# Swapping which down-projection units use paired result banks, spreading the last four activations over four units, and sharing the last stores between two queues

## The chip, the cores and the metric

The kernel runs on one core of a Trainium2 chip. A core has a matrix engine (PE, with its weight loads listed as PEld), a vector engine (DVE), an activation engine (ACT), a GpSimd engine (POOL) and a SyncE queue (SP) that here only issues DMA transfers. Each engine works through its own instructions in order and waits on semaphores for the others. Matrix products land in eight result banks on chip, which PE writes and DVE or ACT read; everything else lies in the big on-chip memory or in device memory.

The metric is the device time of one execution in microseconds. It is 2808.09 us for this kernel, the median of three runs (2815.43, 2808.08 and 2808.09).

## The reference, cut to what matters

One layer of a streaming encoder for 512 prompt frames and 64 sample frames: modulated norms, a token mixer with two kinds of recurrence, and a feed-forward part. Only the feed-forward part and the final norm matter here:

```python
def conv_ffn(h, st, w_up, ffn_conv_w, ffn_conv_b, w_down):
    gate, val = jnp.split(h @ w_up, 2, axis=-1)
    gate_c, new_st = causal_dwconv(gate, st, ffn_conv_w)
    act = jax.nn.silu(gate_c + ffn_conv_b) * val
    return act @ w_down, new_st
...
    x = x + g2 * f
...
    y = rmsnorm(x, final_norm)
```

`w_up` is 2048 x 11264, `w_down` is 5632 x 2048, all in float32. The results are `y_prompt` (512 x 2048), `y_sample` (64 x 2048) and the new states.

## The kernel before, in words

**Float32 by parts.** Each operand of a product is split into a rounded part and a rest. The rounded part is made by ACT (`wh`, line 1630), the rest by a subtraction on DVE (`wl`, line 1632), and a product of two split operands is three matmuls: lines 1725, 1726 and 1727 for the projections of the feed-forward part, lines 647 and 649 elsewhere.

**Units.** The up- and the down-projection use a two-by-two Strassen-Winograd scheme with seven products (`c` = 0 to 6) per unit. Units `t` = 0 to 43 are the up-projection (`NFF` = 44). Units 44 to 75 are the down-projection: four groups `g` = 0 to 3 of eight units `u` = 0 to 7, where a group takes ten of the 44 slices of 128 activations and a unit takes one pair of 128-wide output columns. A product of the down-projection is 5 x 3 matmuls. The products of unit `t` are issued in the order 0, then product 6 of unit `t` - 1, then 2, 1, 3, 4, 5 (`DOWN_ORDER`); unit 44 has no such guest, so its products 0 and 2 stand next to each other.

**Result banks.** A unit has three results x, y, z. Products 0 and 3 go to x, products 2, 4 and 6 to y, products 1 and 5 to z. All up units, and the even down units, take three single banks from `bank()`, which has four of them (tile name `bank`). The odd down units take two tiles from `pgt()`, each a pair of banks (tile name `g`): x and y are the two halves of the first pair, z is half of the second. `pgt()` has two such pairs and serves the stage after the down-projection too. After each product `down_out` adds the result to an output tile: ACT copies (line 1919) where the target is new, which is so in group 0 alone, and DVE adds (line 1921) elsewhere. A later product may write a tile only after that. The framework that orders the instructions follows the priority of the written order, lets a ready instruction go first where one ahead of it isn't ready by its own estimate, and puts in the semaphore waits.

**Weights.** Two steps ahead of each product `up_prep` and `down_prep` make its `wh` and `wl`; DVE also forms the sums that the scheme needs (lines 1643, 1685, 1697 and 1700). The raw weights are loaded by SP (line 1622) into a ring of eight tiles (`raw_late`, list `raws`).

**Places.** The split activations that the products read lie in tiles called `slot`; a list `vacant` keeps the free places. In group 3 no further group is to be loaded, so `vacant` grows: it has nine entries when unit 69 begins and ten at unit 71.

**Group 3.** When a unit of group 3 is complete, `down_end` closes it in steps during the next unit: SP loads the residual (line 1942), POOL adds the last sums (lines 1943 and 1945), ACT scales (line 1953) and POOL adds the residual (line 1954). POOL has nothing to do in groups 0 to 2.

**Last activations.** The groups cover 40 slices. The last four go through a plain product in `final`. `acts` prepares them in the last unit, u = 7 of group 3, at product 2: for each it takes two vacant places and a tile of the ring, SP loads the slice (line 1963), ACT rounds it (line 1964) and DVE subtracts (line 1965).

**Final.** `final_begin` turns the two new convolution states on PE (line 2044). Then two halves `h` of the frames are done; in each, sixteen column blocks get four plain products into pair tiles from `pgt()` (line 2000), DVE scales and adds them (line 2005), and PE turns four blocks at a time (line 2056) for the final norm (lines 2058 to 2061). At the end of a half each of three blocks of frames (128, 128 and 32 rows) gets its factor, four tiles of it are scaled in turn by DVE (line 2072) and ACT (line 2070), and SP stores each right behind its scaling (lines 2075 and 2077): twelve stores for each half.

Of the kernel before, what the change touches and what calls it, by code (L numbers as in the profile page):

```python
# [21 lines left out]
HP, HS, HT = 256, 32, 288  # L22
NFF = 44
# [32 lines left out]
NPAIR = KD // 2  # L56
# [47 lines left out]
class Kern:  # L104
# [1603 lines left out]
    def up_product(self, t, c):  # L1708

        w = HZ if t < NFF else HT  # L1710
        if c == 0:
            if t < NFF or t % 2 == 0:
                banks = [self.bank()[:, :w] for _ in range(3)]
            else:
                a, b = self.pgt(), self.pgt()
                banks = [a[:, 0, :w], a[:, 1, :w], b[:, 0, :w]]
            self.a[t, "banks"] = banks
            self.a.pop((t - 2, "banks"), None)
        T, (wh, wl) = self.nc.tensor, self.a.pop((t, "w", c))
        ps = self.a[t, "banks"][(0, 2, 1, 0, 1, 2, 1)[c]]  # L1720
        n = NPAIR if t < NFF else NJ
        for j in range(n):
            hi, lo, _ = self.combos[c, j] if t < NFF else self.dn[(t - NFF) // NPAIR, c, j]

            T.matmul(ps, wh[:, j], hi, start=(c < 3 and j == 0), stop=False, skip_group_check=True)  # L1725
            T.matmul(ps, wh[:, j], lo, start=False, stop=False, skip_group_check=True)  # L1726
            T.matmul(ps, wl[:, j], hi, start=False, stop=(j == n - 1), skip_group_check=True)  # L1727
# [62 lines left out]
    def up(self):  # L1790
# [110 lines left out]
    def down_out(self, t, c):  # L1901

        nc = self.nc
        V, A, G = nc.vector, nc.scalar, nc.gpsimd
        g, u = divmod(t - NFF, NPAIR)
        x, y, z = self.a[t, "banks"]
        if g == 0 and c == 0:
            for m in (u, u + NPAIR):
                self.x1[m] = self.slot(self.vacant.pop(0), F32, HT)
            if u % 2 == 0:  # L1910
                self.sums_at = self.vacant.pop(0)
                s = self.slot(self.sums_at, F32, HT)
                self.sums[u], self.sums[u + 1] = s[:, 0], s[:, 1]
                self.sums_place.append(self.sums_at)
        lo, hi, p = self.x1[u], self.x1[u + NPAIR], self.sums[u]
        ps, dst, new = ((x, p, True), (z, hi[:, 1], True), (y, lo[:, 1], True), (x, lo[:, 0], True),
                        (y, hi[:, 1], False), (z, lo[:, 1], False), (y, hi[:, 0], True))[c]
        if g == 0 and new:
            A.activation(dst, ps, AF.Copy)
        else:  # L1920
            V.tensor_tensor(dst, ps, dst, op=ALU.add)  # L1921
        if u == NPAIR - 1:
            if c == 0 and g + 1 < NCH:
                self.want(g + 1)
            self.vacant += [self.dn.pop((g, c, j))[2] for j in range(NJ)]
            self.fill()
        if g == NCH - 1:
            if c == 2 and u == NPAIR - 1:
                self.last_acts = self.acts([self.vacant.pop(0) for _ in range(8)])
            if c == 6:  # L1930
                self.closing = self.down_end(u, lo, hi, p)
            if c in (6, 2, 1, 4):
                next(self.closing, None)
# [20 lines left out]
            G.tensor_tensor(x, x, xt[n], op=ALU.add)  # L1954
        yield

    def acts(self, places):

        nc, out = self.nc, []
        for n in range(4):  # L1960
            raw = self.raw_late()[:, :2 * HT].rearrange("p (h t) -> p h t", h=2)
            hh, hl = [self.slot(places[2 * n + i], F32R, HT) for i in range(2)]
            nc.sync.dma_start(raw, self.actd[NFF - 4 + n])
            nc.scalar.activation(hh, raw, AF.Copy)
            nc.vector.tensor_tensor(hl, raw, hh.bitcast(F32), op=ALU.subtract)
            out.append((hh, hl))
        return out

    def down(self):
        for _ in self.closing:  # L1970
# [8 lines left out]


    def final(self, acts, free):


# [65 lines left out]
    def final_part(self, h, q, blocks):  # L2049

        nc, o = self.nc, self.o
# [12 lines left out]
        for c0, n, y, ms in blocks:  # L2064
            V.tensor_reduce(ms[:n, 4:5], ms[:n, 0:4], axis=mybir.AxisListType.X, op=ALU.add)
            self.rsqrt(ms[:, 5:6], ms[:, 4:5], 1, n)
            for q in range(4):
                t = y[q][:n]
                if q % 2:
                    A.activation(t, t, AF.Copy, scale=ms[:n, 5:6])  # L2070
                else:
                    V.tensor_scalar_mul(t, t, ms[:n, 5:6])
                f = slice(q * 512, (q + 1) * 512)
                if c0 < HP:
                    nc.sync.dma_start(o["y_prompt"][0, h * HP + c0:h * HP + c0 + n, f], t)
                else:
                    nc.sync.dma_start(o["y_sample"][0, h * HS:(h + 1) * HS, f], t)


def layer_kernel(tc, i, o):  # L2080
# [216 lines left out]
```

## Time and profile before

| | |
|---|---|
| median of three runs | 2808.09 us |
| the profiled execution's own time | 2809.85 us |
| its span, first to last instruction | 2808.1 us |
| PE / DVE / ACT / POOL busy | 98% / 81% / 47% / 16% of the span |
| stretch 2272 to 2609 us (groups 0 to 2) | PE 336.12 of 337 us, DVE 262.80 |
| stretch 2609 to 2731 us (group 3) | PE 116.65 of 122 us, DVE 110.00 |
| stretch 2731 to 2797 us (final products) | PE 63.88 of 66 us |
| stretch 2797 to 2808 us (last stores) | PE idle |

The rows of a profile give a line of the kernel, its engine and operation, and `out<-in` by the names of the tiles. A pair tile is called `g`, a single bank `bank`. What stands in square brackets behind a row, or behind a bar in a group, is how long the engine was idle just before it, and what ended that. A matmul shows about 0.30 us, but they are pipelined and follow each other by about 0.13 us.

### The profile page before, as it was taken

To read this page: it belongs to the slowest core of one execution; us is meant where nothing else is said; L and a number is where in the kernel's file an instruction comes from. 1 tells how busy PE (TensorE), PEld (TensorE's weight loads), DVE (VectorE), ACT (ScalarE), POOL (GpSimd) and SP (SyncE) were. 2 spreads that over 40 slices of the span, in tenths; PEclk is the share of its full clock that TensorE was granted. 3 is DMA by queue.
4 is the path that set the end of the run, shared out by engine and by line. 5 is a ranking of instruction groups with operands and counts; after the bars stand their busy time and mean duration, and the time that the engine had idled before them with its cause. 6 is when DMAs were issued, how large, how long until landed. Compare 5 with 4: busy or idle time off the path is not lost.

```text
span 2808.1 us, 52899 instructions
## 1 busy us (share of the span) xinstructions
PE 2748.1 (98%) x20612; PEld 2668.6 (95%) x20612; DVE 2285.0 (81%) x3721; ACT 1314.0 (47%) x2314; POOL 458.7 (16%) x437
## 2 busy tenths in 40 slices
PE   7999999999999999999999999999999999999998
PEld 4799999999999999999999999999999999999997
DVE  4578787787877887678999999999998976888886
ACT  4255555464544442355454544444444444333453
POOL 0001000010000000000333333333333300000240
PEclk9999999999999999999999999999999999999999
DMA  9965455554644657633555555464646594673761
GB/s 304 336 195 158 137 140 144 144 154 133 181 142 122 176 166 211 196 101 114 154 162 158 171 157 177 143 184 142 191 142 183 154 299 150 186 235 101 222 173 69
DMA packets 650719, 478.15 MB, mean 170 GB/s; under 512 B 69962, under 2 KB 577093, under 8 KB 650469
## 3 DMA queue, kind: packets, MB, share of 16 engines
q1 hardware_dynamic: 637364, 461.31, 54.9%
q10 hardware_dynamic: 13104, 13.47, 1.6%
q8 instruction: 162, 2.65, 0.4%
q14 instruction: 89, 0.72, 0.1%
HBM read 397.73 MB, written 76.96 MB: 169 GB/s over the span
## 4 chain that ended last, share of the span: by engine, by line
PE 81%; DVE 8%; DMA 4%; issue 3%; ACT 2%; POOL 1%; SPq 0%; ACTq 0%; DVEq 0%; POOLq 0%
PE g L647 17%; PE bank L1726 14%; PE bank L1725 14%; PE bank L1727 14%; PE g L649 8%; PE bank L2219 4%; PE g L1725 2%; PE g L1727 2%; PE g L1726 2%; DVE acc L2203 2%; PE bank L2215 1%; PE bank L869 1%; DVE wl L1632 1%; DVE wl L2203 1%; DVE m L2179 1%
## 5 line engine op out<-in xcount | busy, mean ns | idle before, releaser
L1726 PE MATMUL bank<-slot,wh 128*128 128x290 f32 (+1 forms) x3024 | 903.3, 299 | 0.0
L1725 PE MATMUL bank<-slot,wh 128*128 128x290 f32 (+1 forms) x3024 | 900.8, 298 | 1.3 <-ACT sqa L1599 1.0
L1727 PE MATMUL bank<-slot,wl 128*128 128x290 f32 (+1 forms) x3024 | 894.7, 296 | 0.5 <-DVE wl L1632 0.4
L1727 PEld LDWEIGHTS bank<-slot,wl 128*128 128x128 f32 x3024 | 576.4, 191 | 1.6 <-DVE wl L1632 1.6
L1726 PEld LDWEIGHTS bank<-slot,wh 128*128 128x128 f32 x3024 | 573.7, 190 | 0.1
L1725 PEld LDWEIGHTS bank<-slot,wh 128*128 128x128 f32 x3024 | 568.7, 188 | 4.4 <-ACT sqa L1599 1.3
L647 PE MATMUL g<-hh,wh 128*128 128x288 f32 x2048 | 473.1, 311 | 1.0 <-ACT ts L2203 0.8
L1630 ACT ACTIVATE wh<-raw 128x1024 fp32r<-128x1024 f32 (+1 forms) x304 | 280.4, 923 | 363.1 <-PE bank L1726 263.0
L649 PE MATMUL g<-hh,wl 128*128 128x288 f32 x2048 | 441.9, 297 | 1.7 <-DVE wl L1027 1.7
L647 PE MATMUL g<-hl,wh 128*128 128x288 f32 x2048 | 442.4, 297 | 0.0
L1632 DVE TENSOR_TENSOR wl<-raw,wh 128x1024 fp32r<-128x1024 f32 (+1 forms) x304 | 371.4, 1222 | 73.0 <-ACT wh L1630 69.4
L1630 ACT ACTIVATE wh<-s 128x1024 fp32r<-128x1024 f32 (+1 forms) x228 | 210.7, 926 | 290.4 <-DVE s L1643 103.3
L647 PEld LDWEIGHTS g<-hh,wh 128*128 128x128 f32 x2048 | 325.2, 190 | 21.8 <-issue 15.1
L649 PEld LDWEIGHTS g<-hh,wl 128*128 128x128 f32 x2048 | 330.6, 189 | 5.1 <-issue 3.1
L647 PEld LDWEIGHTS g<-hl,wh 128*128 128x128 f32 x2048 | 330.6, 189 | 3.2 <-issue 2.3
L1632 DVE TENSOR_TENSOR wl<-s,wh 128x1024 fp32r<-128x1024 f32 (+1 forms) x228 | 250.4, 1100 | 14.5 <-ACT wh L1630 13.5
L2203 ACT ACTIVATE wh<-raw 128x1024 fp32r<-128x1024 f32 x135 | 142.6, 1057 | 197.6 <-PE g L647 193.9
L2203 DVE SCALAR_TENSOR_TENSOR acc<-aw,ct,acc 128x512 f32<-128x512 f32 x284 | 201.2, 744 | 3.1 <-DMA aw<-in_w_ada_dram 3.0
L2203 DVE TENSOR_TENSOR wl<-raw,wh 128x1024 fp32r<-128x1024 f32 x135 | 164.8, 1222 | 47.1 <-ACT wh L2203 44.3
L1849 POOL TENSOR_TENSOR j<-j,j 128x288 f32<-128x288 f32 (+1 forms) x120 | 184.4, 1543 | 85.6 <-ACT j L1853 83.1
L1725 PE MATMUL g<-slot,wh 128*128 128x288 f32 x560 | 167.1, 299 | 3.8 <-DVE slot L1921 3.8
L1726 PE MATMUL g<-slot,wh 128*128 128x288 f32 x560 | 165.4, 296 | 0.0
(341 smaller groups left out, 4061.8 us busy)
## 6 DMA issues: line engine op xcount, KB each, us to landing
raw<-in_w_up_dram SPq DMA_DIRECT2D x176, 512.0 KB
raw<-in_w_in_dram SPq DMA_DIRECT2D x100, 512.0 KB
raw<-in_w_down_dram SPq DMA_DIRECT2D x128, 320.0 KB
aw<-in_w_ada_dram SPq DMA_DIRECT2D x79, 512.0 KB
slot<-cd SPq DMA_DIRECT2D x140, 288.0 KB
cd<-j SPq DMA_DIRECT2D x120, 288.0 KB
xr<-in_w_ada_dram SPq DMA_DIRECT2D x49, 512.0 KB
hraw<-in_w_ada_dram SPq DMA_DIRECT2D x40, 512.0 KB
```

The source lines that it names most:

```text
L647: T.matmul(ps[:, h if bank is None else bank, :n], wh, x[:, h, :n], start=f, stop=False)
L649: T.matmul(ps[:, h if bank is None else bank, :n], wl, ah[:, h, :n], start=False, stop=stop)
L869: T.matmul(ps[32 * k:32 * k + 32, :w], cs[:, k0 + k], got[n][k // per][:, k % per], start=(k0 == 0), stop=(k0 == KD - 4))
L1630: self.nc.scalar.activation(hi, src, AF.Copy)
L1632: self.nc.vector.tensor_tensor(lo, src, hi.bitcast(F32), op=ALU.subtract)
L1725: T.matmul(ps, wh[:, j], hi, start=(c < 3 and j == 0), stop=False, skip_group_check=True)
L1726: T.matmul(ps, wh[:, j], lo, start=False, stop=False, skip_group_check=True)
L1727: T.matmul(ps, wl[:, j], hi, start=False, stop=(j == n - 1), skip_group_check=True)
L1849: minus = lambda out, a, b: G.tensor_tensor(out, a, b, op=ALU.subtract)
L2179: return f(*a, **kw)
L2203: return f(*a, **kw)
L2219: return self.engine.matmul(out, *a, **kw)
```

## The change

- `up_product`: of the down units, the even ones now take the pair tiles and the odd ones the single banks. The number of units of either kind stays at sixteen. The first down unit (44) has pairs, the last (75) single banks.
- `act` takes the place of `acts`. It prepares one of the last four slices in each of the units u = 3, 4, 5 and 6 of group 3 (units 71 to 74), again at product 2. The raw slice goes to one of two vacant places used in turn, not to a tile of the weights' ring; the two places are given back after the fourth. ACT's rounding is now put behind the latest rounding of weights on ACT's queue. The instructions are the same four loads, four roundings and four subtractions.
- `final_part`: the scalings of all three blocks are written first and then the twelve stores. In the second half, five stores (the four of the 32-row block and the last of the second block) are issued by ACT, seven by SP. In the first half all twelve stay on SP.

```diff
-            if t < NFF or t % 2 == 0:
+            if t < NFF or t % 2:
                 banks = [self.bank()[:, :w] for _ in range(3)]
             else:
                 a, b = self.pgt(), self.pgt()
...
-        self.closing = iter(())
+        self.closing, self.last_acts = iter(()), []
...
-            if c == 2 and u == NPAIR - 1:
-                self.last_acts = self.acts([self.vacant.pop(0) for _ in range(8)])
+            if c == 2 and u >= 3 and u < NPAIR - 1:
+                self.last_acts.append(self.act(u - 3))
...
+    def act(self, n):
+
+        nc = self.nc
+        if n == 0:
+            self.act_places = [self.vacant.pop(0) for _ in range(2)]
+        raw = self.slot(self.act_places[n % 2], F32, HT)
+        hh, hl = [self.slot(self.vacant.pop(0), F32R, HT) for i in range(2)]
+        nc.sync.dma_start(raw, self.actd[NFF - 4 + n])
+        with self.tc.issue_after(self.round_of):
             nc.scalar.activation(hh, raw, AF.Copy)
+        nc.vector.tensor_tensor(hl, raw, hh.bitcast(F32), op=ALU.subtract)
+        if n == 3:
+            self.vacant += self.act_places
+        return hh, hl
...
+        for k, (c0, n, y, ms) in enumerate(blocks):
+            for q in range(4):
+                t = y[q][:n]
+                queue = nc.scalar if h == 1 and (k == 2 or (k, q) == (1, 3)) else nc.sync
                 f = slice(q * 512, (q + 1) * 512)
                 if c0 < HP:
-                    nc.sync.dma_start(o["y_prompt"][0, h * HP + c0:h * HP + c0 + n, f], t)
+                    queue.dma_start(o["y_prompt"][0, h * HP + c0:h * HP + c0 + n, f], t)
                 else:
-                    nc.sync.dma_start(o["y_sample"][0, h * HS:(h + 1) * HS, f], t)
+                    queue.dma_start(o["y_sample"][0, h * HS:(h + 1) * HS, f], t)
```

More of the change, by code (lines that the diff above doesn't have):

```diff
@@ L1955, in down_end @@
         yield
[L1957 to L1963, printed above, removed]
+    def act(self, n):
[6 more added lines that the diff above has]
+        with self.tc.issue_after(self.round_of):
             nc.scalar.activation(hh, raw, AF.Copy)
-            nc.vector.tensor_tensor(hl, raw, hh.bitcast(F32), op=ALU.subtract)
-            out.append((hh, hl))
-        return out
+        nc.vector.tensor_tensor(hl, raw, hh.bitcast(F32), op=ALU.subtract)
+        if n == 3:
+            self.vacant += self.act_places
+        return hh, hl
     def down(self):
```

## The prediction

> **What bounds the kernel now.** I read the page, then stretches by unit, then what PE waits for from 2600 us on, then the single rows around those waits. Nothing ahead of unit 44 (2272 us) is touched.
>
> ```profile
> PE 2748.1 (98%) x20612; PEld 2668.6 (95%) x20612; DVE 2285.0 (81%) x3721; ACT 1314.0 (47%) x2314; POOL 458.7 (16%) x437
> ```
>
> PE is the bound, so only time in which PE stands can be won. The next view has the stretches of units 69 to 74 one by one, and then unit 75 (columns: us; busy PE, PEld, DVE, ACT, POOL; granted clock; DMA share and GB/s).
>
> ```profile
> 2623.00:2638.00 15.00, 14.43 (x106) 13.86 (x105) 14.69 (x18) 6.67 (x11) 6.35 (x4) 1.00 0.58 158
> 2638.00:2652.00 14.00, 14.00 (x108) 14.00 (x107) 13.97 (x20) 6.89 (x11) 6.95 (x4) 1.00 0.53 136
> 2652.00:2667.00 15.00, 14.45 (x108) 14.12 (x107) 12.90 (x19) 6.88 (x11) 6.38 (x4) 1.00 0.50 128
> 2667.00:2681.00 14.00, 14.00 (x107) 14.00 (x107) 14.00 (x20) 6.89 (x11) 6.95 (x4) 1.00 0.53 138
> 2681.00:2696.00 15.00, 14.45 (x108) 14.12 (x107) 12.91 (x19) 6.88 (x11) 6.37 (x4) 1.00 0.50 128
> 2696.00:2710.40 14.40, 14.02 (x106) 13.79 (x105) 13.87 (x19) 8.05 (x14) 6.51 (x4) 1.00 0.48 129
> 2710.40:2731.40 21.00, 17.30 (x123) 16.23 (x123) 17.61 (x25) 13.26 (x21) 6.15 (x4) 1.00 0.80 233
> ```
>
> Units 70 and 72 (single banks) take 14 us with DVE busy throughout; 71 and 73 (pairs) take 15, PE stands for 0.55, and DVE comes out with about 2 us to spare. What PE waits for from 2600 us to the end (a last row of 0.2 us is left out), and the rows of five of these waits:
>
> ```profile
> PE g L1725 <- DVE slot L1921: 3.8, 5, 1.6
> PE g L647 <- DVE slot L1921: 1.5, 1, 1.5
> PE bank L1727 <- DVE wl L1632: 0.4, 1, 0.4
> ...
> 2631.80 0.37 PE L1725 MATMUL g<-slot,wh 128*128 128x288 f32 x1 [0.56 <-DVE slot L1921]
> 2656.78 0.37 PE L1725 MATMUL g<-slot,wh 128*128 128x288 f32 x1 [0.55 <-DVE slot L1921]
> 2716.32 0.37 PE L1725 MATMUL g<-slot,wh 128*128 128x288 f32 x1 [1.56 <-DVE slot L1921]
> 2721.16 0.37 PE L1725 MATMUL g<-slot,wh 128*128 128x288 f32 x1 [0.61 <-DVE slot L1921]
> 2731.41 0.51 PE L647 MATMUL g<-slot,wh 128*128 128x288 f32 x2 [1.54 <-DVE slot L1921]
> ```
>
> Only pair tiles (`g`) wait for the adding (L1921), never single banks: x and y share a tile, so product 2 waits until product 0 has been added, with one product (2 us) in between as cover. In single banks a result is next written two or three products later. The fifth wait of the 3.8 is unit 73's, 0.55 by the equal stretch. The pool is 3.8 + 1.5 + 0.4 = 5.7 us.
>
> Why the adding is late, in DVE's and POOL's rows at unit 71, and the last activations:
>
> ```profile
> 2654.95 1.32 DVE L1700 TENSOR_TENSOR s<-raw,s 128x640 f32<-128x640 f32 x1
> 2656.19 0.45 DVE L1921 TENSOR_TENSOR slot<-g,slot 128x288 f32<-128x288 f32 x1
> ...
> 2654.26 1.32 POOL L1943 TENSOR_TENSOR slot<-slot,slot 128x288 f32<-128x288 f32 x1 [2.61 <-DVE slot L1921]
> ...
> 2707.52 0.74 DVE L1965 TENSOR_TENSOR slot<-raw,slot 128x576 fp32r<-128x576 f32 x1
> 2718.66 1.98 DVE L1965 TENSOR_TENSOR slot<-raw,slot 128x576 fp32r<-128x576 f32 x1
> ...
> 2718.09 1.94 POOL L1945 TENSOR_TENSOR slot<-slot,slot 128x576 f32<-128x576 f32 x1 [2.96 <-DVE slot L1921]
> ...
> L1965 DVE TENSOR_TENSOR slot<-raw,slot 128x576 fp32r<-128x576 f32 x4 | 4.9, 1213 | 0.5 <-ACT slot L1964 0.5
> L1964 ACT ACTIVATE slot<-raw 128x576 fp32r<-128x576 f32 x4 | 2.7, 686 | 5.4 <-DMA raw<-actd 5.4
> ```
>
> The same subtraction takes 0.74 us alone and 1.98 us where a POOL instruction runs, ending 0.6 us after POOL does. Four of them take 4.9 us, all around unit 75, where the longest wait is.
>
> **The change part by part.**
>
> *Parity in group 3.* Units 69, 71, 73 and 75 lose their pairs and 68, 70, 72 and 74 get them. Unit 68 comes before POOL starts closing units, so nothing is late there: 0. For 70, 72 and 74 the row nearest is unit 71's 0.55 each, since DVE's work per unit doesn't depend on where results lie: 1.65 us come back. Bounds: 0, since a single-bank unit might leave DVE less behind, and 1.56, the worst of unit 75.
>
> *Activations.* One subtraction goes into each of the units 71 to 74. In 72 and 74 (now pairs) it comes at product 2, behind the wait, where DVE has its 2 us to spare: 0; without that spare room 0.74 each. In 71 and 73 (now single banks) DVE has nothing to spare, so it makes the next pair unit's wait 0.74 longer each: 1.5 us. The bounds for each of the four are 0 and 1.98. The roundings (0.69 on ACT, busy 7 of 14 us) and loads lie beside other work; without ACT's room they would add 0.69 each. What DVE loses around unit 75 is 4.9 us, and with single banks there the cover of the adding is two products; so the 1.56, the 0.61 and the 0.4 go. What is late next is the weights' rest (L1632), which stands in the same queue; I take 0 for it in unit 75 and 0.4 (its wait now) as its upper bound.
>
> *Start of `final`.* Its first products take a pair, which unit 74 has left long before; the 1.5 goes. What is late next is the first weights. Their tiles of the ring aren't taken by activations any more, so they load earlier: 0.
>
> Group 3 together: 1.65 + 1.5 - 5.7 = -2.55, and I add -0.35 for two pauses fewer, as PE also loses some 0.16 us in refilling at each (the matmul behind a pause shows 0.37 and not 0.30, and its successor is late too; this is my estimate): **-2.9 us**. Bounds: -5.7, and 1.65 + 4 x 1.98 - 5.7 = +3.9.
>
> *Start of the down-projection.* Unit 44 gets pairs, has no guest product, and its adding is a copy on ACT that stands behind other ACT work:
>
> ```profile
> 2274.46 0.30 PE L1725 MATMUL bank<-slot,wh 128*128 128x288 f32 x1
> 2276.46 0.29 PE L1725 MATMUL bank<-slot,wh 128*128 128x288 f32 x1
> 2277.01 0.40 PE L1727 MATMUL bank<-slot,wl 128*128 128x288 f32 x1
> ...
> 2276.15 0.38 ACT L1919 ACTIVATE slot<-bank 128x288 f32<-128x288 f32 x1
> 2276.14 0.82 DVE L1632 TENSOR_TENSOR wl<-s,wh 128x640 fp32r<-128x640 f32 x1
> ```
>
> Product 2 began at 2274.46 and product 1 at 2276.46. With pairs product 2 can't begin before product 0's copy ends at 2276.53: 2.07 us later. Product 1, in the other pair, could go first, but its rest of weights is ready only at 2276.96, so that way doesn't help much. What goes in return is product 1's own wait for that rest (2277.01 instead of 2276.73, 0.28). Upper bound 2.1; lower 0, if the new order has the copy ahead on ACT. I take **+1.3**, nearer to the upper end, which is the row. The other pair units of groups 0 to 2 have one product of cover as now; no row shows a wait there, and their number is the same: 0.
>
> *Stores.* The last twelve on SP, what feeds them, and the DMA engines in steps of 1 us:
>
> ```profile
> 2798.95 4.48 SPq L2075 DMA_DIRECT2D out_dram<-y  x8
> 2803.53 2.18 SPq L2077 DMA_DIRECT2D out_dram<-y  x4
> ...
> 2798.44 3.78 ACT L2070 ACTIVATE y<-y,fms 128x512 f32<-128x512 f32 x6 [1.71 <-POOL fms L2233]
> ...
> 2800.00:2801.00 1.00, 0.00 (x0) 0.00 (x0) 0.89 (x3) 1.00 (x3) 0.00 (x0) 0.50 1.01 379
> 2804.00:2805.00 1.00, 0.00 (x0) 0.00 (x0) 0.00 (x0) 0.00 (x0) 0.00 (x0) 0.50 1.01 385
> 2805.00:2806.00 1.00, 0.00 (x0) 0.00 (x0) 0.00 (x0) 0.00 (x0) 0.00 (x0) 0.50 0.96 281
> 2806.00:2807.00 1.00, 0.00 (x0) 0.00 (x0) 0.00 (x0) 0.00 (x0) 0.00 (x0) 0.50 0.44 100
> ```
>
> Issuing ends at 2805.71. With seven on SP (2798.95 + 7 x 0.56 = 2802.9) and five on ACT behind its scalings (2802.2 + 5 x 0.55 = 2805.0, or less), issuing ends 0.7 us earlier or more. But the transfers fill the DMA engines from 2800 to 2806; only the 0.04 and 0.56 us unused in the last two steps can go. So **-0.5 us**, between 0 and -0.6.
>
> The Trainium skill ("DMA: Bandwidth & Descriptors", section "Issuing engines are not separate DMA queues") says that transfers from any issuing engine run on the same sixteen DMA engines and that several issuers save only issue time. By issue time alone the sum would have -0.7 here; the share of 1.01 agrees with the page that there is no more to get.
>
> In the first half the stores come behind all scalings in the written order; SP has nothing else there, and other products run meanwhile: 0, or up to 0.56, one issue, if a tile that is to be written again has to wait for its store.
>
> Sum: -2.9 + 1.3 - 0.5 = **-2.1 us**. Against the profiled execution (2809.85, span 2808.1) that is 2807.75; that execution lies 1.8 us above the median 2808.09, so I predict 2806.0.
>
> **The rivals.**
>
> *All of group 3's waits go* (DVE places the subtractions in its gaps, and 70, 72 and 74 don't wait): -5.7 + 1.3 - 0.5 = -4.9, so 2803.2. For it: DVE's 2 us to spare in pair units. Against: 13.97 and 14.00 of 14 in the others.
>
> *DVE becomes the bound in units 71 to 74*, slower than before. All four subtractions are paid in full, at the mean of 1.21 us: 1.65 + 4.85 - 5.7 + 1.3 - 0.5 = +1.6, so 2809.7; at 1.98 each +4.7, so 2812.8. It decides from (5.7 - 1.65 - 1.3 + 0.5) / 4 = 0.81 us paid for each. For it: DVE's stretches above, POOL busy 6.4 to 7 of each 14. Against: the number of POOL instructions that can hold up DVE stays the same. A rule of the Trainium skill ("SBUF — State Buffer", section "Who interferes with whom") bears on it: a DVE instruction with two SBUF inputs and a GpSimd one that reads SBUF exclude each other for a whole instruction. The 1.98 us row agrees; by that rule each subtraction that meets L1945 costs what that row shows.
>
> *SP's queue gets stuck.* A load of an activation that waits for its place holds up the weights behind it. SP's waits and ACT's for weights:
>
> ```profile
> SPq L1963 <- DVE wl L1632: 9.5, 3, 3.9
> ...
> L1630 ACT ACTIVATE wh<-raw 128x640 fp32r<-128x640 f32 x128 | 94.5, 739 | 149.6 <-PE g L1726 81.5 <-PE bank L1726 54.1 <-DVE wl L1632 7.1
> ```
>
> Now such loads wait up to 3.9 us on SP. Four of these fully paid would be +15.6 - 2.1 = +13.5, so 2821.6. Against: the new places are free two units before, and no large share of ACT's idle time for weights is ended by a DMA, so the weights come early enough.
>
> **How the numbers follow.** The forecast has 0.5, all waits gone 0.2, DVE as the bound 0.2, the queue 0.1. The range 2801.5 to 2811.5 takes in the forecast, the first rival with its cheapest start (2803.2 - 1.3), and the second up to 1.7 us for each subtraction; the forecast's own range is 2804 to 2808. A measurement of this kernel can tell about 0.3%, 8.4 us, from no change. More than that is won in no case worked out here (5.7 + 0.6 at most), but I leave 0.04; lost only with the queue, 0.10; within it 0.86.
>
> **What would show it.** In the changed profile PE's waits for L1921 should be about three, at pair units 70, 72 and 74, of 0.5 to 1.4 us; none between the last product of unit 75 and the first of `final`; a new wait of 1 to 2 us near 2274 for L1919; the subtractions in four different units; five stores on ACT, the DMA engines full until the same stretch, and the last landing about 0.5 us earlier behind the last scaling. It is wrong if PE waits for `wl` (L1632) in single-bank units 71 and 73, if ACT's idle time before L1630 is ended by a DMA, or if the schedule of unit 44 is another.

## The result and the profile after

The changed kernel takes 2818.27 us (median of 19 runs, 2812.72 to 2822.47) against 2809.84 us for the kernel before (19 runs on the same chip, 2805.21 to 2818.55). The ratio is 1.0028, with a 95% interval from 1.0021 to 1.0034: slower by 8 us. The prediction had 2806.0 us and a range up to 2811.5.

To see where the time went, both profiled executions are cut at places that every variant has: the start of unit 44's first product, of unit 68's, of unit 69's, of `final`'s first product (L647) and of its second half's, the end of PE's last matmul, and the end of the span. The first half of `final` also holds the transposes that run between its products. Before unit 44 the code is untouched, and what differs there (2272.48 and 2270.78 us) is noise.

| us | 44 to 68 | 68 | 69 to `final` | `final`, first half | second half | after PE | from 44 on |
|---|---|---|---|---|---|---|---|
| before | 336.47 | 13.95 | 108.51 | 30.37 | 33.80 | 12.55 | 535.7 |
| changed | 337.78 | 14.11 | 109.28 | 35.19 | 33.78 | 12.63 | 542.8 |
| difference | +1.3 | +0.2 | +0.8 | **+4.8** | 0 | +0.1 | **+7.1** |
| forecast | +1.3 | 0 | -2.9 | 0 | 0 | -0.5 | -2.1 |

PE's total on the page has hardly changed (the kernel before had 2748.1):

```profile
PE 2747.9 (98%) x20612; PEld 2666.7 (95%) x20612; DVE 2285.6 (81%) x3721; ACT 1313.7 (47%) x2314; POOL 458.9 (16%) x437
```

What PE waits for from 2200 us to the end of the changed kernel (us in total, times, longest):

```profile
PE g L1725 <- DVE slot L1921: 4.6, 3, 1.6
PE g L647 <- DVE slot L2008: 3.5, 2, 3.3
PE bank L1725 <- ACT hw L2031: 1.1, 1, 1.1
PE g L1725 <- ACT slot L1919: 1.1, 1, 1.1
```

The three waits at the pair units are where the prediction put them, but of 1.49 to 1.57 us each. Together with a new 1.08 at unit 75's last product they make 5.7 us up to `final`: as much as the pool of 5.7 that was to shrink to 3.15. And a wait of 3.3 us stands in `final`, where none was forecast. The rows of the pair units and of that wait:

```profile
2643.08 0.37 PE L1725 MATMUL g<-slot,wh 128*128 128x288 f32 x1 [1.49 <-DVE slot L1921]
2673.25 0.37 PE L1725 MATMUL g<-slot,wh 128*128 128x288 f32 x1 [1.56 <-DVE slot L1921]
2703.77 0.37 PE L1725 MATMUL g<-slot,wh 128*128 128x288 f32 x1 [1.57 <-DVE slot L1921]
...
2738.26 0.81 PE L647 MATMUL g<-slot,wh 128*128 128x288 f32 x2 [3.28 <-DVE slot L2008]
```

**The pair waits.** Engines by stretch, units 70 to 73, each from the start of a unit (columns: us; busy PE, PEld, DVE, ACT, POOL; granted clock; DMA share and GB/s), then the subtractions of the activations (before: x4, 4.9 us) and one of them beside POOL's instruction:

```profile
2637.40:2653.30 15.90, 14.41 (x108) 14.08 (x107) 13.78 (x20) 6.88 (x11) 6.36 (x4) 1.00 0.47 123
2653.30:2667.60 14.30, 14.26 (x107) 14.02 (x107) 14.30 (x19) 7.46 (x12) 7.07 (x4) 1.00 0.57 153
2667.60:2684.10 16.50, 14.78 (x107) 14.04 (x107) 16.43 (x22) 7.45 (x12) 6.58 (x4) 1.00 0.52 136
2684.10:2698.10 14.00, 14.00 (x108) 14.00 (x107) 14.00 (x18) 7.46 (x12) 6.64 (x4) 1.00 0.51 136
```
```profile
L1967 DVE TENSOR_TENSOR slot<-slot,slot 128x576 fp32r<-128x576 f32 x4 | 8.0, 1993 | 0.0
...
2674.28 1.95 POOL L1945 TENSOR_TENSOR slot<-slot,slot 128x576 f32<-128x576 f32 x1 [2.23 <-DVE slot L1921]
...
2674.86 1.99 DVE L1967 TENSOR_TENSOR slot<-slot,slot 128x576 fp32r<-128x576 f32 x1
```

In unit 72 (74 is like it) the 2 us that DVE had to spare are gone: 16.43 us busy of 16.50. Each of the four subtractions takes 1.99 us, since each now meets POOL's L1945 and ends 0.6 us behind it. The 1.98 that the prediction kept for an upper bound is what all four cost. The Trainium skill ("SBUF — State Buffer", section "Who interferes with whom") says that a DVE instruction with two SBUF inputs contends with a GpSimd one that reads SBUF, and that the ports they share are an exclusive lock; the trace agrees with 1.99 against 0.74 us, and also in that the adding from PSUM (L1921, one SBUF input) takes 0.44 to 0.46 us in all its 184 rows, beside POOL or not.

**The wait in `final`.** The rows of ACT, POOL and DVE that lead to 2738.26, and ACT's of the kernel before at the same place:

```profile
2734.18 0.96 ACT L1953 ACTIVATE slot<-slot,mod 128x512 f32<-128x512 f32 x2 [2.00 <-POOL slot L1943]
2735.04 1.04 ACT L2210 ACTIVATE wh<-raw 128x1024 fp32r<-128x1024 f32 x1
...
2732.41 1.73 POOL L1943 TENSOR_TENSOR slot<-slot,slot 128x288 f32<-128x288 f32 x1 [1.73 <-DVE slot L1921]
...
2736.12 1.54 DVE L2210 TENSOR_TENSOR wl<-raw,wh 128x1024 fp32r<-128x1024 f32 x1 [1.89 <-ACT wh L2210]
2737.57 0.63 DVE L2008 SCALAR_TENSOR_TENSOR slot<-g,mod,slot 128x256 f32<-128x256 f32 x2
```
```profile
2727.46 2.00 ACT L2203 ACTIVATE wh<-raw 128x1024 fp32r<-128x1024 f32 x2
2730.19 1.06 ACT L2203 ACTIVATE wh<-raw 128x1024 fp32r<-128x1024 f32 x1 [0.73 <-DMA raw<-in_w_down_dram]
2732.25 0.96 ACT L1953 ACTIVATE slot<-slot,mod 128x512 f32<-128x512 f32 x2 [1.00 <-POOL slot L1943]
```

L2210 (L2203 before) is the rounding of `final`'s first weights, and L1953 the scaling in unit 75's closing. Before, all three roundings stood ahead of the scaling. Now the third stands behind it, on the same queue; the scaling waits for POOL; DVE's subtraction of these weights waits for the rounding; and `final`'s adding (L2008), which frees the pair tile that PE is to write next, is queued behind that subtraction. The third load isn't late: SP issues it at 2716.64, before at 2726.55. The diff doesn't touch one of these lines. The order on a queue is worked out when the kernel is built, and it came out another way.

**The clock.** The stretch with the wait and the one behind it:

```profile
2734.92:2738.33 3.41, 0.13 (x2) 0.07 (x1) 2.09 (x3) 1.68 (x3) 3.06 (x2) 1.00 0.72 229
2738.33:2741.75 3.42, 3.42 (x15) 3.42 (x15) 0.17 (x1) 2.81 (x6) 1.89 (x2) 0.50 0.00 1
```

Behind the pause the granted clock is 0.50 until 2741.75, and a matmul follows the last by 0.24 us in place of 0.13. That makes the other 1.5 us of the 4.8.

### The profile page after: what moved, and what is told of

The parts are those of the page before. It is cut to its first block, busy times and chain, and to the rows that moved or that the text cites. A ratio compares the mean times of both kernels' runs of the same rounds, so it can differ in the third digit from the quotient of the medians.

```text
span 2813.5 us, 52896 instructions
## 1 busy us (share of the span) xinstructions
PE 2747.9 (98%) x20612; PEld 2666.7 (95%) x20612; DVE 2285.6 (81%) x3721; ACT 1313.7 (47%) x2314; POOL 458.9 (16%) x437
## 4 chain that ended last, share of the span: by engine, by line
PE 82%; DVE 8%; issue 3%; DMA 3%; ACT 2%; POOL 1%; SPq 0%; ACTq 0%; POOLq 0%; DVEq 0%
PE g L647 17%; PE bank L1726 14%; PE bank L1725 14%; PE bank L1727 14%; PE g L649 8%; PE bank L2226 4%; PE g L1725 2%; PE g L1727 2%; PE g L1726 2%; DVE acc L2210 2%; PE bank L2222 1%; PE bank L869 1%; DVE wl L2210 1%; DVE wl L1632 1%; DVE m L2186 1%
## 5 line engine op out<-in xcount | busy, mean ns | idle before, releaser
L647 PE MATMUL g<-hh,wh 128*128 128x288 f32 x2048 | 473.4, 312 | 1.9 <-ACT ts L2210 1.7
L647 PE MATMUL g<-hl,wh 128*128 128x288 f32 x2048 | 442.4, 297 | 0.0
L647 PEld LDWEIGHTS g<-hh,wh 128*128 128x128 f32 x2048 | 325.6, 190 | 22.6 <-issue 15.1
L647 PEld LDWEIGHTS g<-hl,wh 128*128 128x128 f32 x2048 | 330.5, 189 | 3.6 <-issue 2.7
L2210 ACT ACTIVATE wh<-raw 128x1024 fp32r<-128x1024 f32 x135 | 142.7, 1057 | 201.1 <-PE g L647 198.0
L2210 DVE SCALAR_TENSOR_TENSOR acc<-aw,ct,acc 128x512 f32<-128x512 f32 x284 | 201.7, 746 | 3.4 <-DMA aw<-in_w_ada_dram 3.3
L2210 DVE TENSOR_TENSOR wl<-raw,wh 128x1024 fp32r<-128x1024 f32 x135 | 164.9, 1221 | 48.7 <-ACT wh L2210 46.3
```

Source lines behind the costliest of these rows:

```text
L647: T.matmul(ps[:, h if bank is None else bank, :n], wh, x[:, h, :n], start=f, stop=False)
L2210: return f(*a, **kw)
```

## The experiments

All stage times are those of the table above, from each variant's own profiled execution; the ratio is to the kernel before in the same session.

### The parts one by one

**The pairs alone.**

```diff
-            if t < NFF or t % 2 == 0:
+            if t < NFF or t % 2:
```

> The pairs alone, activations and stores as before. Common to both theories: the first products of unit 44 come about 1.5 us later than before, and the order on ACT puts the third rounding of the first weights of `final` behind the first half of unit 75's scaling, which waits for POOL, so PE should wait some 3 us in `final`. Theory 1 (DVE lacks time in group 3, PE's waits at the pairs are that lack): units 70, 72 and 74 have no subtraction of an activation in or before them, so the waits are about 1.1 us at 70 (the lack of 69 and 70) and 0.55 to 1.1 us at 72 and 74, 2.2 to 3.3 us together; sum +1.5 +3 and at most 1 us for the rest: 3 to 5.5 us slower than before. Theory 2 (the cover of the whole-tile wait is short in even units, whatever DVE has to do): 1.5 us at each of the three, 4.6 us together, 5 to 7 us slower.

2815.19 us, ratio 1.0015 (1.0007 to 1.0024). From unit 44 on 540.0 us: +4.4. By stages: 338.49, 14.11, 107.81, 33.29, 33.78, 12.55. The waits at the pair units:

```profile
2646.89 0.37 PE L1725 MATMUL g<-slot,wh 128*128 128x288 f32 x1 [1.49 <-DVE slot L1921]
2675.72 0.37 PE L1725 MATMUL g<-slot,wh 128*128 128x288 f32 x1 [0.55 <-DVE slot L1921]
2704.55 0.37 PE L1725 MATMUL g<-slot,wh 128*128 128x288 f32 x1 [0.54 <-DVE slot L1921]
2713.08 0.40 PE L1725 MATMUL g<-slot,wh 128*128 128x288 f32 x1 [1.04 <-DVE slot L1921]
...
2740.05 0.54 PE L647 MATMUL g<-slot,wh 128*128 128x288 f32 x2 [2.74 <-DVE slot L2005]
```

At their product 2 units 72 and 74 wait for 0.55 us, as the prediction had taken it from unit 71's row; only unit 70 has 1.49. A likely reason is that units 69 and 70 both come behind and that there is no wait at 69 in which DVE catches up, but no run isolates it. So the even units as such don't cost 1.5 us each. A fourth wait, 1.04 us late in unit 74, comes behind two of the four subtractions: written for unit 75, they run at 2706.56 and 2711.90 here. The expectation had no subtraction in or before unit 74. From unit 69 to `final` this part alone wins 0.7 us. The wait in `final` is there too (2.74), and the start of the down-projection is late.

**The activations alone**: the new `act` and its call, with the pairs as before.

```diff
-            if c == 2 and u == NPAIR - 1:
-                self.last_acts = self.acts([self.vacant.pop(0) for _ in range(8)])
+            if c == 2 and u >= 3 and u < NPAIR - 1:
+                self.last_acts.append(self.act(u - 3))
```

> The four activations alone, one each in units 71 to 74; pairs in odd units and stores as before. Theory 1 (DVE's lack): each subtraction that meets POOL's adding costs DVE 1.99 us, so the waits at the pair units 71, 73 and 75 grow from 0.55 to 1.5 us or more, 4 us or more together. Theory 2 (the cover in even units): 0.55 us at 71 and 73 as before and 0.6 or less at 75. Common: unit 44 as before; a wait of about 3 us in `final`, since the order on ACT has the third rounding behind unit 75's scaling here too. Sum by theory 1: 2 to 5 us slower than before; by theory 2: 0 to 2 us slower.

2810.88 us, ratio 1.0001 (0.9992 to 1.0010); from unit 44 on 538.2 us, +2.6. By stages: 337.17, 13.95, 108.29, 32.50, 33.77, 12.55.

```profile
2653.82 0.37 PE L1725 MATMUL g<-slot,wh 128*128 128x288 f32 x1 [0.54 <-DVE slot L1921]
2684.33 0.37 PE L1725 MATMUL g<-slot,wh 128*128 128x288 f32 x1 [1.52 <-DVE slot L1921]
2714.82 0.37 PE L1725 MATMUL g<-slot,wh 128*128 128x288 f32 x1 [1.53 <-DVE slot L1921]
2728.22 0.50 PE L647 MATMUL g<-slot,wh 128*128 128x288 f32 x2 [0.77 <-DVE slot L1921]
2733.39 0.30 PE L2059 MATMUL bank<-consts,slot 128*128 128x128 f32 x1 [1.75 <-DVE slot L2008]
```

The wait at unit 73 goes from 0.55 to 1.52 us; the one at 75 stays where it was, at 1.53 (1.56 before, behind the subtractions that stood there). Against the pairs alone the changed kernel's waits at 72 and 74 go from 0.55 to 1.57 in the same way. It is the subtraction in the unit before, and not the parity, that adds 1 us to each. `final` again loses 2.1 us, behind a wait of 1.75 where about 3 were expected.

**The stores alone**: the changed end of `final_part`, with its stores behind all scalings.

```diff
+                queue = nc.scalar if h == 1 and (k == 2 or (k, q) == (1, 3)) else nc.sync
...
-                    nc.sync.dma_start(o["y_prompt"][0, h * HP + c0:h * HP + c0 + n, f], t)
+                    queue.dma_start(o["y_prompt"][0, h * HP + c0:h * HP + c0 + n, f], t)
```

> The last stores alone: five from ScalarE, all behind the scalings. The traces of before and of the changed kernel have 12.55 and 12.63 us from PE's last product to the end, so 0.0 to +0.1 us, and a ratio of 1.000. The prediction's step said -0.5. If the issuing on SP had been the limit, -0.7 or more.

2810.45 us, ratio 1.0005 (0.9996 to 1.0013); 12.68 us from PE's last product to the end, against 12.55 before. Nothing is won. ACT's and SP's stores in this run:

```profile
2798.80 4.35 SPq L2079 DMA_DIRECT2D out_dram<-y  x7
...
2802.05 3.25 ACTq L2081 DMA_DIRECT2D out_dram<-y  x3
```

The last three take 3.25 us of ACT's queue, 1.1 each, where the prediction had taken 0.55. Issuing ends at 2805.30, 2.8 us ahead of the end, and before it was 2.4 (2805.71 of 2808.14).

The three parts alone make 4.4 + 2.6 + 0.2 = 7.2 us by their traces, against 7.1 in the changed kernel. But the sums agree only in total. From unit 69 to `final` the parts make -0.7, -0.2 and -0.2 us and the changed kernel has +0.8, so their meeting costs 1.9 us there. From unit 44 to 68 the parts make 3.0 us against 1.3; this stretch holds units 44 and 45, which take 27.0 to 29.8 us over the traces.

**Unit 44 on single banks.**

```diff
-            if t < NFF or t % 2:
+            if t <= NFF or t % 2:
```

> The changed kernel with unit 44 on single banks (unit 46 is the first with pairs). The wait of 1.06 us for ScalarE's copy goes, and the time from the first product of unit 44 to that of unit 45 falls from 14.1 to 12.3 to 13.2 us, as in the kernels with pairs in odd units: 1 to 1.7 us faster than the changed kernel. If the late start were the pairs' in general, unit 46 would show the wait instead. The rest as in the changed kernel: three waits of 1.5 us, 3.3 us in `final`.

From unit 44 to 68 336.72 us against 337.78: the wait for ACT's copy is gone and unit 46 has none. Unit 44 takes 11.95 us in place of 14.05, but unit 45 then takes 15.04 in place of 13.96, with a wait of 0.76 us for weights that the kernel before has there too. Over all traces the six kernels with pairs in unit 44 take 338.3 us on average in this stretch (337.7 to 339.6), the seven with pairs in odd units 336.9 (336.1 to 337.7).

Most of that difference isn't unit 44's. From unit 46 to 68 all seven kernels with pairs in even units take 309.7 to 309.8 us, this run among them, and the seven with pairs in odd units 308.9 to 309.0 (309.3 with all activations in unit 68). In the changed kernel unit 61 holds most of it (14.76 us against 14.10 before), with two short pauses from 2513.88 on; why they come is open. The rest of this run is as in the changed kernel, with a wait of 3.27 us in `final` and the slow matmuls behind it once more (36.22 us for the first half), and its total, 2815.55 us (1.0015, 1.0006 to 1.0024), is less of a difference than the measurement can carry.

### What makes DVE late

**The changed kernel without POOL's closing additions.**

```diff
-        G.tensor_tensor(lo[:, 1], lo[:, 1], p, op=ALU.add)
...
-        G.tensor_tensor(hi, hi, p.unsqueeze(1).to_broadcast([P, 2, HT]), op=ALU.add)
...
-            G.tensor_tensor(x, x, xt[n], op=ALU.add)
```

> The changed kernel without POOL's four additions that close each unit of group 3 (the sum p and the residual are left out, so y is not the reference's). Theory 1 (DVE's lack, made by POOL): the four subtractions take 0.74 us each, and the waits at 70, 72 and 74 fall from 1.5 to under 0.3 us each. Theory 2 (cover): these waits stay at 1.5 us. By the theory on the order, the 3.28 us in `final` go too, as the scaling waits for POOL no more. Sum: 5 to 9 us faster than the changed kernel by theory 1, 3 to 4 by theory 2.

2807.10 us, ratio 0.9988 (0.9979 to 0.9997). From unit 69 to `final` 101.37 us in place of 109.28. From 2640 to 2790 us a single row is left of PE's waits, and the subtractions (L1964 here) take 0.75 us:

```profile
PE g L647 <- DVE slot L2005: 1.6, 2, 1.4
...
L1964 DVE TENSOR_TENSOR slot<-slot,slot 128x576 fp32r<-128x576 f32 x4 | 3.0, 752 | 0.0
```

The pairs and their short cover are the same, and no pair waits. Theory 2 of the first runs, that the cover alone makes the waits, falls. From unit 44 on it is 11.3 us less than in the changed kernel, more than was expected; of the wait of 3.28 us in `final` 1.39 stay, where none was expected.

**All four activations in unit 68**, before POOL has anything to close, in the kernel before.

```diff
-            if c == 2 and u == NPAIR - 1:
+            if c == 2 and u == 0:
```

> The kernel before with all four activations in unit 68, before POOL's closing work begins. Theory 1: each subtraction takes 0.74 us, where DVE has time to spare; waits at 71 and 73 stay at 0.55 us, the 1.56 at 75 falls to about 0.55, the 1.5 us at the start of `final` goes; 1 to 3 us faster than before. A rival: the loads of the activations in the ring hold up unit 68's weights on SP, and PE waits in unit 68 for weights, 1 to 4 us, which gives it back.

2820.50 us, ratio 1.0037 (1.0025 to 1.0050): 10 us slower. The subtractions take 0.75 us, as expected, and the waits at 71 and 73 stay at 0.58 and 0.54, but that at 75 is 1.66 where 0.55 was expected. From unit 69 to `final` there are 113.38 us, and another 2.9 us are lost in the first half of `final`. PE's new waits in units 69 and 70, and what stands before them:

```profile
2618.19 5.44 SPq L1963 DMA_DIRECT2D raw<-actd  x4
2627.12 2.91 DVE L1965 TENSOR_TENSOR slot<-raw,slot 128x576 fp32r<-128x576 f32 x4
2645.62 0.82 DVE L1643 TENSOR_TENSOR s<-raw,raw 128x640 f32<-128x640 f32 x1 [0.76 <-DMA raw<-in_w_down_dram]
...
2630.82 0.40 PE L1727 MATMUL g<-slot,wl 128*128 128x288 f32 x1 [1.33 <-DVE wl L1632]
2636.60 0.40 PE L1725 MATMUL g<-slot,wh 128*128 128x288 f32 x1 [1.79 <-ACT wh L1630]
2648.21 0.40 PE L1725 MATMUL bank<-slot,wh 128*128 128x288 f32 x1 [1.85 <-ACT wh L1630]
```

The first wait isn't the rival's. The four subtractions stand in one row on DVE, 2.91 us in unit 69, and the rest of the weights that ends the wait stands behind them. The wait of 1.85 us comes behind a load: DVE stands until the weights land at 2645.62. That agrees with the rival, and with the prediction's third one, but whether the activations' loads on SP or the tiles of the ring that they took made it late is not shown. The clock falls to 0.50 behind the second wait (last section).

**The closing additions of units 68 to 74 on DVE**, in the kernel before.

```diff
-        A, G = nc.scalar, nc.gpsimd
+        A, G = nc.scalar, nc.vector if u < NPAIR - 1 else nc.gpsimd
```

> The kernel before with the four closing additions of units 68 to 74 on DVE instead of POOL (unit 75's stay on POOL). Without them DVE was busy for 11.5 to 12.1 us of each unit's 14, and beside POOL for 13.0 to 14.0: being shut out costs it about 2 us per unit. Doing the work itself costs it 0.45 + 3 x 0.74 = 2.67 us. Theory 1 (PE's waits are what DVE lacks): DVE is at its limit again, 14.1 of 14 us, and units 69 to 75 get 0 to 5 us longer than before. Theory 2 (waits come from how late single POOL instructions make one adding): no instruction is stretched to 1.3 or 2 us any more, the waits go, and these units get 2 to 5 us shorter.

2808.77 us, ratio 0.9987 (0.9978 to 0.9997): a little faster than before, and by the two ratios (0.9987 and 1.0028) 0.4% faster than the changed kernel. From unit 69 to `final` 102.97 us, 5.5 less; the first half of `final` gives 1.8 of it back. PE's waits from 2640 to 2790 us (a last row of 0.4 us is left out), one wait ahead of them, and the stretch of units 70 to 73, before and here:

```profile
PE g L647 <- DVE slot L2005: 0.7, 2, 0.5
PE g L649 <- DVE wl L2203: 0.7, 1, 0.7
PE g L1725 <- ACT wh L1630: 0.7, 1, 0.7
...
2635.94 0.37 PE L1725 MATMUL g<-slot,wh 128*128 128x288 f32 x1 [0.64 <-DVE slot L1921]
...
2638.12:2695.78 57.66, 56.56 (x422) 55.91 (x421) 53.45 (x73) 27.53 (x44) 26.64 (x16) 1.00 0.52 133
2640.02:2696.11 56.09, 56.09 (x423) 55.84 (x422) 53.45 (x90) 27.55 (x44) 0.00 (x0) 1.00 0.51 137
```

From unit 70 on no pair waits for the adding any more; unit 69's still does, for 0.64 us. In units 70 to 73 DVE is busy for 53.45 us in both kernels: the additions cost it as much time when POOL does them, by the stretching, as when it does them itself. With the same busy time the waits are gone, so theory 1 falls in the form in which it was put to this run (DVE's total work is the limit). That points to where the stretched instructions stand: 1.3 or 2 us at a place behind which an adding is due. It is not the whole cause, as the wait at unit 69 and the next run show.

**The changed kernel with the closing on DVE**, and the order at the end mended as in the next run.

> The changed kernel with the closing additions of units 68 to 74 on DVE, and the first three weights of `final` ahead of unit 75's scaling; pairs, activations and stores as changed. If the stretched instructions make the waits (theory 2 of the run before, in its milder form): no wait over 0.3 us at units 70, 72 and 74, the four subtractions 0.75 us each, 101.5 to 103.5 us from unit 69 to `final` against 109.3 in the changed kernel, 31 to 32.5 us for the first half of `final`; unit 44 keeps its 1.3 us; from unit 44 on 531.5 to 534 us, a ratio of 0.998 to 0.9995 to before. If DVE's total work decides (theory 1), its 2.67 us for the closing and 0.74 us for a subtraction bring units 71 to 74 over 14 us each, and waits of 0.5 us or more come at 72 and 74: over 105 us there, and no faster than before.

2807.37 us, ratio 0.9991 (0.9982 to 1.0000). From unit 69 to `final` 103.22 us in place of 109.28; the subtractions take 0.75 us. What PE waits for from 2640 to 2790 us:

```profile
PE g L1725 <- ACT wh L1630: 1.9, 3, 0.6
PE g L647 <- DVE slot L2010: 1.2, 2, 1.0
```

The adding ends no wait. In its place three waits of 0.6 us for ACT's rounding of weights have come, at units 70, 72 and 74, where none over 0.3 was expected. The rows show DVE behind them: its sum (L1700) for unit 72 ends at 2683.14, ACT rounds that sum from 2683.26 to 2684.00, and PE goes on at 2684.03; units 70 and 74 are alike. So with a subtraction in each unit DVE's own work does hold PE up, by 0.6 us and not by 1.5. The first half of `final` takes 31.39 us.

### The order at the end

**The first three weights ahead of unit 75's scaling**, in the changed kernel. `final_w` then takes the tiles from `self.first`.

```diff
+        self.first = [self.wtile(self.w_down(NFF - 4, m)) for m in (0, 2, 4)]
+        self.round_of = self.nc.cur_bb.bb.instructions[-2]
         for _ in self.closing:
             pass
```

> The changed kernel, with the first three weights of `final` written ahead of the rest of unit 75's closing, and that closing's scaling held behind the third rounding on ACT; nothing else moves. Theory on the order: the third rounding no longer stands behind a scaling that waits for POOL, so PE's wait of 3.28 us falls to 1 us or less, the clock stays at 1.00 after it, and the first half of `final` takes 30.4 to 32.0 us in place of 35.2: 3 to 5 us faster than the changed kernel, 1.0010 to 1.0018 of before. Rival: the third weights' load is late by itself (POOL and the stores of residuals aside), then the wait stays at 2 us or more and the gain is under 2 us.

2814.36 us, ratio 1.0015 (1.0006 to 1.0024). The first half of `final` takes 32.52 us in place of 35.19, and the wait falls from 3.28 to 1.81 us, with the clock at 1.00 behind it. From unit 44 on that is 2.9 us less. So the order costs 2.7 of the 4.8 us, the clock included. It doesn't explain all: ACT's third rounding still stands behind two roundings of later weights, which wait for their load.

```profile
2734.05 1.15 ACT L2033 ACTIVATE hw<-raw 128x512 fp32r<-128x512 f32 x2 [0.66 <-DMA raw<-in_w_down_dram]
2735.11 1.04 ACT L2212 ACTIVATE wh<-raw 128x1024 fp32r<-128x1024 f32 x1
```

**The same, and the activations' raw tiles in the ring again.**

```diff
-        raw = self.slot(self.act_places[n % 2], F32, HT)
+        raw = self.raw_late()[:, :2 * HT].rearrange("p (h t) -> p h t", h=2)
```

> The changed kernel with the order at the end mended as in the run above, and with the activations' raw tiles from the ring again instead of two vacant places. The step of the prediction on the start of `final` held that giving the ring's tiles back costs nothing. Theory: giving them back let three loads of later weights run ahead, so that their roundings on ACT came between those of the first weights; with the ring the six roundings come before product 6's, as in the kernel before. Then the wait of 0.78 us at unit 75's last product goes, the wait of 1.81 us in `final` falls under 0.5, and the first half of `final` takes 30.3 to 31 us: 2 to 3 us faster than the run above without the ring. Rival: DVE's subtractions at the end decide, whatever ACT's order; then a wait of 1.5 us stays in `final` or at its start.

2814.03 us, ratio 1.0016 (1.0007 to 1.0025): no gain over the run above. The wait in `final` falls to 0.49 us and its first half to 31.34, as expected, but unit 75's last product now waits 1.87 us for DVE's adding, and a wait of 1.07 for weights has come at unit 73's last product: unit 69 to `final` is 110.66 us in place of 109.03. Behind the 1.87 us the granted clock is 0.50 from 2732.84 to 2736.25, which costs about half of that time, 1.7 us by estimate. What ACT's order gives, DVE's late adding and the clock take back, so the rival held here. The subtractions take 1.11 and three times 0.75 us in this run, and the pairs still wait 1.49, 1.66 and 0.90 us: less stretching of the subtractions alone doesn't end the waits.

**The kernel before with one activation per unit, once in units 68 to 71 and once, from the ring, in 71 to 74**, the end mended in both. The first:

```diff
+            if c == 2 and u < 4:
+                self.last_acts.append(self.act(u))
```

The second is the run with the activations alone, with `raw_late` for their raw tiles.

> The kernel before (pairs in odd units, stores as before) with one activation in each of the units 68 to 71, two before POOL has anything to close, and the three first weights ahead of unit 75's scaling. By DVE's lack: two subtractions at 0.74 us in time to spare; waits at 71 of 0.6 to 1.5 us, at 73 and 75 of 0.55 each, at the start of `final` 0.8 or less; the first half of `final` 30.4 to 31.5 us: 2 to 4 us faster than before (ratio 0.9985 to 0.9993). If the loads of the activations hold up weights on SP as with all four in unit 68, waits for weights appear in units 68 to 71, and it is the same as before or slower.

> Pairs in odd units and stores as before, one activation in each of the units 71 to 74 with raw tiles from the ring, the first three weights ahead of unit 75's scaling. By DVE's lack waits of 0.55, 1.5 and 1.5 us stay at 71, 73, 75 and 0.8 at the start of `final`; the first half of `final` takes 30.3 to 31 us. From unit 44 on 535 to 536.5 us against 535.7 before: the same within 0.1%. Faster than before by more than 2 us only if the waits shrink as well.

2811.36 us (1.0005, 0.9996 to 1.0013) and 2809.49 us (0.9999, 0.9990 to 1.0008). The first has pair waits of 1.52 (unit 69), 1.56 (71) and twice 0.54, and one of 0.20 for weights in units 68 to 71, but 32.22 us for the first half of `final`; from unit 44 on 538.2 us, 2.6 more than before where 2 to 4 less were expected. Unit 69's wait was 0.56 before, and its two subtractions take 0.75 us each: DVE had no time to spare for them there, stretched or not. The second has 535.2, as expected, but not by the waits that were expected: 0.54, 0.89 and 0.92 at units 71, 73 and 75 in place of 0.55, 1.5 and 1.5. Spreading the activations, with any of these orders, wins nothing that could be measured.

## Why the prediction was wrong

*The pair units.* The mechanism was right: waits at 70, 72 and 74, for the adding, and the subtractions of 71 and 73 paid at the next pair unit. The size was off. The subtractions were counted at 0.74 us; the instruction takes 1.99 at all four places, as in the row of before at unit 75. Left on its own the parity costs 0.55 at product 2 of 72 and 74, as forecast, and 1.49 at 70, where the lack of unit 69 had been counted as gone. The 3.7 us between -2.9 and +0.8 are made up as follows, to within 0.3 us, by the distances from one matmul's start to the next. Unit 70's wait is 0.94 longer than forecast. The subtractions of 71 and 73 add 1.0 to the next pair's wait and not 0.74: 0.55 for both. Unit 75's last product waits 1.08, where "I take 0 for it in unit 75" stood; ACT's queue was held there by a rounding of later weights (L2031, 2726.61) that waited 3.26 us for its load. "In 72 and 74 (now pairs) it comes at product 2, behind the wait, where DVE has its 2 us to spare: 0" was too low by 0.5 each: the wait at 74 is no longer than that at 72, but about 6 us behind either two matmuls follow the last by 0.3 and 0.4 us in place of 0.13 (2679.62 and 2680.26). Two short pauses of the same kind stand in unit 69, 0.6 us, as in all kernels with pairs in even units. The refilling came nearly as forecast: with four long waits in place of seven it is about 0.45 us less.

*Unit 75 and the start of `final`.* The 1.56, 0.61, 0.4 and 1.5 did go. But "what is late next is the first weights ... so they load earlier: 0" failed, and it is the largest error: +4.8 us in the first half of `final`. Not the load was late but the rounding, by its place on ACT's queue behind a scaling that waits for POOL. The mended order gives 2.7 us back, the clock included. What remains, about 2 us, is of the same kind as the 1.5 that had gone: wherever the order was mended, a wait of 0.5 to 1.9 us for DVE or for a rounding stayed in unit 75 or near `final`'s start.

*The start of the down-projection.* +1.3 was forecast and +1.3 measured, but that is luck. The wait for the copy on ACT came as told (1.06 us) and is gone with single banks in unit 44. Unit 44 takes 14.05 us in place of 12.32, but unit 45 takes 13.96 in place of 15.24, as weights that PE had to wait for are ready by then: +0.45 for both. The other 0.85 stand in units 46 to 67, for which the prediction had 0.

*The stores.* -0.5 was forecast, +0.1 measured. The reason given against a gain (the DMA engines are full) was right, but the gain of issue time counted on 0.55 us for a store from ACT, and the last three took 1.1 each.

*The rivals.* "DVE becomes the bound" has the right mechanism for group 3 and, with 2812.8 us at 1.98 for each, it came nearest; it was outside the range, since 1.7 was taken as the most. But its four subtractions paid in full are not what the traces show (1.0 us for two of them, 0.5 for the others), and the largest loss lay in `final`. SP's queue was not stuck in the changed kernel. No rival had the order of ACT's queue at the start of `final`.

## What to carry to other kernels

Before an instruction is moved to where an engine "has time", look at what else runs there: if a row of the trace shows it stretched beside another engine's instruction, take the stretched time. A change of tiles or of a step's place can give another order on a queue that it doesn't touch: compare the order of each engine's instructions near the critical places, and ask of each one that waits what stands behind it. Work that shuts out another engine may cost that engine as much as the work itself: here the busy engine was busy for 53.45 us over four units, whether the idle engine did the sixteen additions or it did them itself, and in the second case no matmul of these units waited for its adding.

## What was not expected of the hardware

One pause of 3.28 us was enough to halve the granted clock for 3.41 us, 2.74 us with the pairs alone left it at 1.00, and with all activations in unit 68 it fell behind a wait of only 1.79 us. The times of the changes show why the length of the pause doesn't decide. In each trace they lie a multiple of 3.41 us apart (in the changed kernel 2738.33, 2741.75 and 2803.19). Cut by this grid, the stretches with the 2.74 us (the first two rows) and those around the fall behind 1.79 us are:

```profile
2735.45:2738.87 3.42, 1.86 (x15) 1.63 (x13) 1.77 (x5) 2.35 (x4) 2.72 (x3) 1.00 0.94 202
2738.87:2742.28 3.41, 2.23 (x17) 2.23 (x18) 1.39 (x4) 0.41 (x2) 3.01 (x2) 1.00 0.98 305
...
2634.50:2637.91 3.41, 1.61 (x13) 1.38 (x12) 2.90 (x4) 2.10 (x4) 0.52 (x1) 1.00 0.40 94
2637.91:2641.33 3.42, 3.42 (x17) 3.42 (x16) 1.40 (x3) 0.86 (x2) 1.32 (x1) 0.50 0.79 209
```

The pause of 2.74 us lies across an edge of the grid, so PE is busy for 1.86 us in one stretch and for 2.23 in the next; the 1.79 us lie within one stretch, with 1.61 busy. From 2210 us on, over all fourteen traces, each stretch with 1.80 us or more of idle PE was followed by half the clock. Of those with less one was (1.48 us, with the ring, at 2275.45), and others of up to 1.79 us were not. So the limit lies near half a stretch, as far as these traces tell; the ends of matmuls are modelled, and what it is exactly stays open.

The Trainium skill ("TensorE: Matmul & The Clock Gate", section "Part 1: The HAM clock gate (the "warmup" mystery)") says that the clock is halved after an idle window of about 3.4 us, and given back after a busy one of that length, in windows that run on their own. The grid of 3.41 us agrees with it, and so does the way back: half the clock lasts for one busy stretch here, and for two (6.83 us) in the run with unit 44 on single banks, where PE stood for 0.82 us of the first. But the window need not be idle as a whole. The time lost is that of the pause and about half of the slow stretch, 1.5 us here.
